# A two-block transformer and SSM kernel on one core: normed activations at another distance from the weights modulo 256 bytes, with three edits to the first layer and the SSD decays

## The chip, the core and the metric

The kernel runs on one core of one Trainium2 chip, in one launch. The metric is the device time of a launch in microseconds. All numbers of the profile are of one profiled execution.

## What is computed

The input `x` is 256 tokens of width 1024, in float32, with a context `ctx` of 256 tokens. Two blocks follow each other:

```
def first_block(x, ...):                 # two layers, h = h + layer(rms_norm(h))
    even: q, k, v, gate_a, u, gate_b = split(hn @ w_in)
          att = swa_sink_attention(rms(q), rms(k), v) * silu(gate_a)
          ssm = s5_mixer(u, log_dt, a, b, c, ...) * silu(gate_b)   # scan, then GLU
          out = concat(att, ssm) @ w_out
    odd:  q, k, v, gate, qi, ki, wi = split(hn @ w_in)
          out = (dsa_attention(q, k, v, qi, ki, wi) * silu(gate)) @ w_out

def second_block(x, c, ctx, c_ctx, ...):  # two layers, each: mixer, then a SwiGLU FFN
    sh1, sc1, g1, sh2, sc2, g2 = split(silu(c) @ ada_w + ada_b)    # and for ctx by c_ctx
    h = rmsnorm(x) * (1 + scale) + shift
    layer 0: attention of x over x and ctx (and of ctx over itself)
    layer 1: SSD mixer: z, xbc, dt = split(h @ w_in); conv; per head, in both
             directions, y = sum_j exp(-|cum_i - cum_j|) dt_j (C_i B_j) x_j + ...
    x = x + g1 * mixer;  x = x + g2 * swiglu(modulate(rmsnorm(x)))
    return rmsnorm(x)
```

`cum` is the running sum of `dt * A` of a head, `A = -exp(A_log)`. The weights come to about 260 MB in float32, and each is used once.

## The kernel before

**Dense products.** A weight tile `raw` of [128, 1024] float32 comes by DMA from SP. `Weights.load` (L171) splits it in two: ScalarE rounds it to `h` (L178), VectorE subtracts to get the rest, `l` (L179; GpSimd does so for the first `on_pool` tiles of a stage, counts in the list `LP`). The activations are split in the same way into H and L tiles of [128, 8, 256] (`nhx`, `nlx` for x, `nhc`, `nlc` for ctx, out of `norm_T`, L311; `yH`, `yL`, `oH`, `oL` out of the mixers; `fh`, `fl` within an FFN). Each product is then three matmuls: h with H, h with L, and l with H. All of them are recorded on line 129, in `mm`, so the tiles tell them apart. There are two forms. In the feature form (`feat_tiles`, L271) the weights are the stationary operand, and 256 columns of the activations move: `pu`, `pg`, `pffnx`, `pffnc`, `pcvx`. In the token form (`tok_step`, L229) a [128, 128] piece of the activations is stationary, and 256 or 512 columns of the weights move: `pdx`, `pdc`.

**Addresses.** Each partition holds its tiles at a fixed byte address. Modulo 256, the weights `h` and `l` lie at 224, the normed activations and the mixers' outputs at 160, an FFN's `fh` and `fl` at 160 (x) and 32 (ctx), the SSD's `ysH` at 32.

**Stages.** The even layer runs to about 330 us, with the adaLN rows (`pada`, from 512 KB tiles `araw` or `aw` of `ada_w`) and the ctx half of the second block's first layer in its holes; the odd layer to 515; the ctx FFN and the attention of x to 800; the first FFN of x to 1001; the SSD mixer `x_ssm` to 1362; the second FFN to 1557. What each engine does next is fixed in its own list of instructions by a scheduler, which goes by the program's order and by priorities; a `with after(mark)` holds what stands in it behind a marked instruction.

**First layer.** `norm_T` transposes x (`pntx`) and writes `nhx` (ScalarE, L334) and `nlx` (VectorE, L335). `late_params` (L358) brings small parameters into the tile `rp`, `A_log` among them, and makes `A = -exp(A_log)` by a power on GpSimd (L378) and steps L379 to L381 on VectorE. The S5 set-up makes its rotation tables from 16-column angle tiles `sv` on VectorE (L475 to L517, then `bb`, `bd`), and six table products `tabs` per quarter on GpSimd (L647 to L652). `cond_columns` (L860) makes `cT`, the silu of c and c_ctx, which every `pada` matmul needs; it is called at the head of `ctx_start`.

**SSD.** For each of eight groups of four heads, `project(g)` makes x, B and C (`pcvx`, then the convolution `cv`, `fT`) and z. `decay_rows(g)` fetches the rows of `cum` for the group into tiles `D_`, one per chunk of 128 tokens, and `decays(g)` makes the decay factors EW from them on GpSimd and ScalarE. It runs one group ahead:

```
G.tensor_tensor(D_, D_, negc[:, c, g, :, None] ..., op=ALU.subtract)   # L1396, 128x1024
S.activation(D_, D_, AF.Relu, scale=-1.0)                              # L1398, 128x1024
G: W = msk * dt (L1402, twice), W + Wb (L1403); E = D_0 + D_1 (L1405)
S.activation(E, E, AF.Exp, scale=-1.0)                                 # L1406
G.tensor_tensor(EW, E, W, op=ALU.mult)                                 # L1408
```

Ahead of some norms, a few warm matmuls (512 columns of float32 constants, counted as `pntx`) keep TensorE busy while it waits: two before the first FFN, five before the SSD, seven before the second FFN.

## Time and profile before

| what | value |
|---|---|
| median of 3 runs | 1563.68 us (1563.24 to 1567.5) |
| profiled execution, its own time | 1568.09 us |
| its span | 1566.3 us, mean granted clock 0.982 |
| TensorE matmul busy | 1484.5 us (95%) |
| VectorE, ScalarE, GpSimd busy | 1110.8, 770.8, 303.5 us (71%, 49%, 19%) |
| DMA | 264.56 MB, mean 169 GB/s |

The span is what the trace covers; the own time is what a launch took on the device. Idle time of an engine matters only where the end waits for it, so the shares are read first, then the chain that ended last, and then, for the stretches in question, busy time, waits and the groups of instructions.

### The profile page before, as it was taken

To read this page: it belongs to the slowest core of one execution; us is meant where nothing else is said; L and a number is where in the kernel's file an instruction comes from. 1 tells how busy PE (TensorE), PEld (TensorE's weight loads), DVE (VectorE), ACT (ScalarE), POOL (GpSimd) and SP (SyncE) were. 2 spreads that over 40 slices of the span, in tenths; PEclk is the share of its full clock that TensorE was granted. 3 is DMA by queue.
4 is the path that set the end of the run, shared out by engine and by line. 5 is a ranking of instruction groups with operands and counts; after the bars stand their busy time and mean duration, and the time that the engine had idled before them with its cause. 6 is when DMAs were issued, how large, how long until landed. Compare 5 with 4: busy or idle time off the path is not lost.

```text
span 1566.3 us, 26965 instructions
## 1 busy us (share of the span) xinstructions
PE 1484.5 (95%) x10560; PEld 1263.1 (81%) x10560; DVE 1110.8 (71%) x1825; ACT 770.8 (49%) x1386; POOL 303.5 (19%) x247
## 2 busy tenths in 40 slices
PE   6799999999999999999989999989899999999998
PEld 5574556786898888687779999888789898699997
DVE  6779996667766778666566666568988876665666
ACT  4433445654554555677444544445455544454444
POOL 2415660000100100000000000148975400200000
PEclk9899999999999999999999999998999999999999
DMA  9684555566665767642666465454544333556664
GB/s 254 228 233 142 184 173 164 139 182 200 200 180 172 223 192 212 217 121 95 209 203 192 162 185 180 141 134 125 125 112 131 105 95 122 159 161 188 193 189 134
DMA packets 306174, 264.56 MB, mean 169 GB/s; under 512 B 27441, under 2 KB 260703, under 8 KB 306048
## 3 DMA queue, kind: packets, MB, share of 16 engines
q1 hardware_dynamic: 306048, 262.85, 56.4%
q8 instruction: 83, 1.36, 0.4%
q14 instruction: 43, 0.35, 0.1%
HBM read 261.47 MB, written 1.34 MB: 168 GB/s over the span
## 4 chain that ended last, share of the span: by engine, by line
PE 78%; DVE 8%; DMA 5%; POOL 4%; ACT 2%; issue 2%; SPq 1%; POOLq 0%; DVEq 0%; ACTq 0%
PE pdx L129 21%; PE pffnx L129 16%; PE pdc L129 8%; PE pffnc L129 7%; PE pcvx L129 5%; PE pada L899 3%; PE pg L129 3%; DMA araw<-ada_w 2%; DVE l L179 2%; PE py L129 1%; PE pocx L129 1%; PE ptcx L1117 1%; PE pv L129 1%; POOL EW L1408 1%; PE pqi L129 1%
## 5 line engine op out<-in xcount | busy, mean ns | idle before, releaser
L179 DVE TENSOR_TENSOR l<-raw,h 128x1024 fp32r<-128x1024 f32 (+2 forms) x366 | 454.2, 1244 | 269.9 <-ACT h L178 239.0
L178 ACT ACTIVATE h<-raw 128x1024 fp32r<-128x1024 f32 (+2 forms) x374 | 389.0, 1042 | 412.3 <-PE pdx L129 103.2
L129 PE MATMUL pffnx<-nlx,h 128*128 128x256 f32 x704 | 169.6, 281 | 0.6 <-DVE nlx L354 0.6
L129 PE MATMUL pffnx<-nhx,h 128*128 128x256 f32 x704 | 169.7, 281 | 0.0
L129 PEld LDWEIGHTS pffnx<-nlx,h 128*128 128x128 f32 x704 | 133.8, 190 | 2.1 <-issue 1.2
L129 PEld LDWEIGHTS pffnx<-nhx,h 128*128 128x128 f32 x704 | 133.9, 190 | 0.5 <-issue 0.4
L308 POOL TENSOR_TENSOR sums<-sums,nhalf 128x1 f32<-128x1 f32 x20 | 13.0, 652 | 538.5 <-DVE sums L304 525.4
L129 PE MATMUL pffnx<-nhx,l 128*128 128x256 f32 x704 | 97.1, 280 | 0.0
L129 PE MATMUL pffnc<-nhc,h 128*128 128x256 f32 x352 | 88.9, 287 | 0.4 <-ACT nhc L353 0.4
L129 PEld LDWEIGHTS pffnx<-nhx,l 128*128 128x128 f32 x704 | 88.4, 189 | 0.8 <-issue 0.8
L129 PE MATMUL pffnc<-nlc,h 128*128 128x256 f32 x352 | 87.9, 285 | 0.1
L179 POOL TENSOR_TENSOR l<-raw,h 128x1024 fp32r<-128x1024 f32 (+1 forms) x8 | 18.5, 2314 | 352.3 <-PE pdx L129 199.5
L129 PE MATMUL pdx<-h,nhx 128*128 128x256 f32 (+1 forms) x256 | 83.3, 343 | 1.8 <-DVE cv L1290 1.8
L899 PE MATMUL pada<-araw,cT 128*32 128x256 f32 x704 | 71.8, 395 | 11.8 <-DMA araw<-ada_w 11.1
L129 PE MATMUL pdx<-h,nlx 128*128 128x256 f32 (+1 forms) x256 | 81.5, 336 | 0.0
L129 PE MATMUL pdx<-h,fh 128*128 128x256 f32 (+1 forms) x264 | 77.2, 318 | 0.0
L129 PE MATMUL pcvx<-nhx,h 128*128 128x256 f32 x256 | 73.5, 297 | 3.8 <-DVE cv L1290 3.8
L129 PE MATMUL pdx<-h,fl 128*128 128x256 f32 (+1 forms) x264 | 77.1, 317 | 0.0
L129 PE MATMUL pcvx<-nlx,h 128*128 128x256 f32 x256 | 71.5, 289 | 0.0
L129 PEld LDWEIGHTS pffnc<-nhc,h 128*128 128x128 f32 x352 | 66.5, 189 | 2.9 <-issue 1.2
L129 PEld LDWEIGHTS pffnc<-nlc,h 128*128 128x128 f32 x352 | 66.5, 189 | 2.1 <-DVE nlc L354 0.5
L129 PE MATMUL pdx<-l,nhx 128*128 128x256 f32 (+1 forms) x256 | 57.2, 338 | 1.4 <-DVE l L179 1.3
(622 smaller groups left out, 3884.2 us busy)
## 6 DMA issues: line engine op xcount, KB each, us to landing
araw<-ada_w SPq DMA_DIRECT2D x88, 512.0 KB
raw<-ffn_w_gate SPq DMA_DIRECT2D x66, 512.0 KB
raw<-ffn_w_up SPq DMA_DIRECT2D x66, 512.0 KB
raw<-ffn_w_down SPq DMA_DIRECT2D x54, 512.0 KB
raw<-ssm_w_in SPq DMA_DIRECT2D x48, 512.0 KB
raw<-od_w_in SPq DMA_DIRECT2D x25, 512.0 KB
raw<-attn_w_qkv SPq DMA_DIRECT2D x24, 512.0 KB
raw<-attn_w_o SPq DMA_DIRECT2D x32, 256.0 KB
```

What stands on the lines that cost most here:

```text
L129: i = T.matmul(out, l, r, start=start, stop=stop)
L178: S.activation(h[:, :n], raw[:, :n], AF.Copy)
L179: (G if self.on_pool > 0 else V).tensor_tensor(l[:, :n], raw[:, :n], h[:, :n].bitcast(F32), op=ALU.subtract)
L308: G.tensor_tensor(s[:, 3:4], s[:, j - 1:j], nhalf[:, 0:1], op=ALU.pow)
L899: T.matmul(pt[32 * q:32 * q + 32, 0:256], cT[:, k, :], raw[:, q * 256:(q + 1) * 256], start=k == 0, stop=k == 7, tile_position=(0, 32 * q))
L1117: T.transpose(pt[:, e, r], P[:, e, r, ki * 128:(ki + 1) * 128], ident)
L1408: G.tensor_tensor(EW, E, W, op=ALU.mult)
```

## The change

It has six parts.

1. **Addresses.** A helper `lane` makes the activation tiles 2112 elements wide, and uses 2048 of them from an offset of 60 (`nhx`, `nlx`, `nhc`, `nlc`) or 36 (`yH`, `yL`, `oH`, `oL`); a `pad` in `con`, and larger `hb`, `sink`, `padf`, `padk`, shift the rest. Modulo 256 the weights stay at 224. The normed activations go from 160 to 144, that is from 64 to 80 bytes below the weights; the mixers' outputs to 48; `fh`, `fl` of x to 32.
2. **First layer.** `cond_columns` is called right behind the first norm; the decay rates' part of `late_params` becomes `decay_rates`, called behind the odd layer; the first quarter's six table products wait for the first head norm's `rstd`.
3. **`LP[5]`** from 4 to 0: the first four `l` splits of the SSD are VectorE's.
4. **SSD decays.** GpSimd's subtraction of `cum` and the Relu become eight Relus of [128, 128] with a bias, and group 0's decays stand behind `project(0)`.
5. **Warm matmuls**: two, five and seven become none, four and six.
6. On SP, the two DMAs of `crows` (c and c_ctx) stand at places 8 and 9 of its list, and stood at 32 and 33; the DMA of `A_log` at 39, and stood at 27.

```
-LP = (0, 0, 2, 0, 2, 4)
+LP = (0, 0, 2, 0, 2, 0)
...
+    con.tile([128, 48], F32, name="pad")
...
+    def lane(tag, name, off):
+        t = act.tile([128, 2112], F32R, tag=tag, name=name)
+        return t[:, off:off + 2048].rearrange("p (k t) -> p k t", k=8)
...
-            G.tensor_tensor(r[:, :cnt], t[:, :cnt], nhalf[:, :cnt], op=ALU.pow)
+            i = G.tensor_tensor(r[:, :cnt], t[:, :cnt], nhalf[:, :cnt], op=ALU.pow)
+        marks.setdefault("rs" + key, i.ins)
...
-          H = act.tile([128, 8, 256], F32R, tag="h" + key, name="nh" + key)
-          L = act.tile([128, 8, 256], F32R, tag="l" + key, name="nl" + key)
+          H = lane("h" + key, "nh" + key, 60)
+          L = lane("l" + key, "nl" + key, 60)
...
+    def decay_rates():
+        ar = con.tile([64, 80], F32, name="ar")
+        a_diag, a_log, a_pos = ar[:, 0:64], ar[:, 64:65], ar[:, 65:67]
         SY.dma_start(a_log, dram(D("ssm_A_log_2"), 0, [[1, 64], [1, 1]]))
         G.tensor_tensor(a_pos[:, 0:1], ebase[0:64, 0:1], a_log, op=ALU.pow)
...
             wx.on_pool = LP[0]
+            cond_columns()
...
-            yH = act.tile([128, 8, 256], F32R, tag="hx", name="yH")
-            yL = act.tile([128, 8, 256], F32R, tag="lx", name="yL")
+            yH = lane("hx", "yH", 36)
+            yL = lane("lx", "yL", 36)
...
+                    with after(None if q else "rshe"):
+                        G.tensor_tensor(ct, hi(cos_), lo(cos_), op=ALU.mult)
...
+        if key == "x":
+            p.tile([128, 32], F32, name="padf")
...
-            ffn(p, wx, xt, i, 0, "x", psx, "xf", (11, 11), amid=amid, warm=(("endo", 2), ("ends", 7))[i])
+            ffn(p, wx, xt, i, 0, "x", psx, "xf", (11, 11), amid=amid, warm=((None, 0), ("ends", 6))[i])
...
-                    G.tensor_tensor(D_.rearrange("p d h i -> p (d h) i"), D_.rearrange("p d h i -> p (d h) i"),
-                                    negc[:, c, g, :, None].to_broadcast([128, 8, 128]), op=ALU.subtract)
-                    S.activation(D_, D_, AF.Relu, scale=-1.0)
+                    for d in range(2):
+                        for h in range(4):
+                            S.activation(D_[:, d, h], D_[:, d, h], AF.Relu, scale=-1.0,
+                                         bias=cum[:, 2 * c + d, 4 * g + h:4 * g + h + 1])
...
-            ew = decays(0, decay_rows(0))
+            row0 = decay_rows(0)
+            ew = None
...
-                EW = ew
+                EW = ew or decays(0, row0)
+    decay_rates()
```

**VectorE at the first norm.** Here `nlx` are the L halves of the first normed activations, `rp` the rates' steps, `sv` and `turn` the S5 angles, `cT` the conditioning columns. Before:

```order
L467 COPY ldx<-ldt 16x128
L335 SCALAR_TENSOR_TENSOR nlx<-pntx,par,nhx 128x256 x4
L471 COPY sv<-psp 128x48
L475 TENSOR_TENSOR sv<-sv 128x16
L480 TENSOR_TENSOR turn<-sv 128x16
L508 TENSOR_TENSOR sv<-sv 128x16
L379 TENSOR_SCALAR rp<-rp 64x1
L481 TENSOR_SCALAR turn<-turn 128x16
L335 SCALAR_TENSOR_TENSOR nlx<-pntx,par,nhx 128x256
L380 SCALAR_TENSOR_TENSOR rp<-rp 64x1
L483 CAST th_h<-turn 128x16
```

and now:

```order
L342 SCALAR_TENSOR_TENSOR nlx<-pntx,par,nhx 128x256
L478 COPY ldx<-ldt 16x128
L342 SCALAR_TENSOR_TENSOR nlx<-pntx,par,nhx 128x256
L883 TENSOR_SCALAR cT<-pcc 128x2x8
L342 SCALAR_TENSOR_TENSOR nlx<-pntx,par,nhx 128x256 x3
L482 COPY sv<-psp 128x48
L486 TENSOR_TENSOR sv<-sv 128x16
L491 TENSOR_TENSOR turn<-sv 128x16
L519 TENSOR_TENSOR sv<-sv 128x16
L492 TENSOR_SCALAR turn<-turn 128x16
L342 SCALAR_TENSOR_TENSOR nlx<-pntx,par,nhx 128x256
L494 CAST th_h<-turn 128x16
```

The steps on `rp` are gone from in front of the last `nlx`, and `cT`, which before stood at row 66 of this list, stands ahead of the last four.

**GpSimd at the same time.** `ldt`, `rp` (now `ar`) and `sv` are powers, `x` and `tabs` the table products, `t` and `r` a head norm's `rstd`. Before:

```order
L464 TENSOR_TENSOR ldt<-ebase,ld 16x2
L378 TENSOR_TENSOR rp<-ebase,rp 64x1
L476 TENSOR_TENSOR sv<-ebase,sv 128x16
L648 TENSOR_TENSOR x_196<-tr 128x512
L647 TENSOR_TENSOR tabs<-tr 128x512
L650 TENSOR_TENSOR tabs<-tr 128x512
L647 TENSOR_TENSOR tabs<-tr 128x512
L650 TENSOR_TENSOR tabs<-tr 128x512
L649 TENSOR_TENSOR tabs<-tabs,x_196 128x512
```

and now:

```order
L475 TENSOR_TENSOR ldt<-ebase,ld 16x2
L487 TENSOR_TENSOR sv<-ebase,sv 128x16
L388 TENSOR_TENSOR ar<-ebase,ar 64x1
L315 TENSOR_TENSOR sums<-sums,nhalf 128x1 x2
L292 TENSOR_SCALAR t<-ss 128x8
L293 TENSOR_TENSOR r<-t,nhalf 128x8
L659 TENSOR_TENSOR tabs<-tr 128x512
L660 TENSOR_TENSOR x_206<-tr 128x512
L662 TENSOR_TENSOR tabs<-tr 128x512
L659 TENSOR_TENSOR tabs<-tr 128x512
```

The power of `A_log` stands behind that of `sv`, and the first head norm ahead of the tables.

**ScalarE in the SSD's first group.** `cv` is the convolution's copy out of `pcvx`, `h` on L178 (now L184) the weights' split, `h_...<-phs` a state, and the `D_` rows are the decays. Before:

```order
L1437 ACTIVATE xf<-pxt 128x256
L1398 ACTIVATE D__10494<-D__10494 128x1024
L178 ACTIVATE h<-raw 128x1024
L1398 ACTIVATE D__10496<-D__10496 128x1024
L1406 ACTIVATE D__10494<-D__10494 128x512
L1362 ACTIVATE h_10832<-phs 128x512
L1287 ACTIVATE cv<-pcvx,par 128x512
L1406 ACTIVATE D__10496<-D__10496 128x512
```

and now:

```order
L1449 ACTIVATE xf<-pxt 128x256
L1368 ACTIVATE bc<-pct 128x128
L184 ACTIVATE h<-raw 128x1024
L1412 ACTIVATE D__10490<-D__10490,cum 128x128 x8
L1412 ACTIVATE D__10492<-D__10492,cum 128x128 x8
L1301 ACTIVATE cv<-pcvx,par 128x512
L1376 ACTIVATE h_10806<-phs 128x512
L1421 ACTIVATE D__10490<-D__10490 128x512
L184 ACTIVATE h<-raw 128x1024
```

Sixteen small Relus in two rows stand together, ahead of `cv` and the state's copy.

## Rows read from the trace of the kernel before

**Rows 1.** The page's first part: busy us, share of the span and instructions of each engine.

```profile
PE 1484.5 (95%) x10560; PEld 1263.1 (81%) x10560; DVE 1110.8 (71%) x1825; ACT 770.8 (49%) x1386; POOL 303.5 (19%) x247
```

**Rows 2.** Waits of TensorE, 0 to 70 us: total, times, longest.

```profile
PE pada L899 <- DVE cT L871: 5.0, 1, 5.0
PE pu L129 <- DVE nlx L335: 4.7, 2, 4.0
```

**Rows 3.** The chain that ended last, first 270 us: start, us, what.

```profile
20.13 2.25 DMA rp<-ssm_A_log
...
54.35 1.40 DVE bd L537
...
217.98 5.50 DMA araw<-ada_w
```

**Rows 4.** Timeline of VectorE: start, us, instruction, in brackets idle before and releaser.

```profile
23.01 0.15 DVE L379 TENSOR_SCALAR rp<-rp 64x1 f32<-64x1 f32 x1 [3.60 <-POOL rp L378]
...
34.41 0.16 DVE L515 TENSOR_TENSOR sv<-sv 128x16 f32<-128x16 f32 x1
...
37.72 0.98 DVE L511 TENSOR_TENSOR sv<-sv 128x16 f32<-128x16 f32 x1
...
43.66 0.17 DVE L871 TENSOR_SCALAR cT<-pcc 128x16 f32<-128x16 f32 x1
```

**Rows 5.** Windows: length; busy PE, PEld, DVE, ACT, POOL; clock, DMA share, GB/s.

```profile
20.00:50.00 30.00, 21.29 (x142) 17.35 (x143) 24.29 (x50) 9.81 (x14) 13.97 (x11) 0.77 0.83 293
50.00:80.00 30.00, 26.76 (x170) 18.64 (x169) 20.12 (x33) 14.28 (x21) 11.41 (x12) 0.89 0.70 221
80.00:108.00 28.00, 28.00 (x219) 24.80 (x218) 17.24 (x23) 12.19 (x14) 3.17 (x4) 1.00 0.85 229
```

**Rows 6.** The same view, windows of the SSD groups.

```profile
1042.00:1062.00 20.00, 15.00 (x97) 13.04 (x96) 13.08 (x19) 9.18 (x17) 12.15 (x9) 0.85 0.68 155
1062.00:1160.00 98.00, 86.91 (x656) 81.46 (x655) 85.75 (x108) 49.55 (x87) 88.54 (x61) 0.98 0.48 125
1160.00:1240.00 80.00, 74.75 (x585) 71.48 (x586) 69.67 (x110) 44.10 (x82) 41.19 (x31) 0.98 0.41 112
1240.00:1310.00 70.00, 70.00 (x561) 67.08 (x560) 54.49 (x99) 35.37 (x71) 7.55 (x8) 1.00 0.33 98
```

**Rows 7.** Lines L1396 and L1398 alone: durations in ns, min/median/max, and start.

```profile
L1396 POOL TENSOR_TENSOR D__10494<-D__10494,cumg x1: 1897/1897/1897, 1047.6 to 1047.6; 128x1024 f32<-128x1024 f32 x1
...
L1396 POOL TENSOR_TENSOR D__10940<-D__10940,cumg x1: 2875/2875/2875, 1090.3 to 1090.3; 128x1024 f32<-128x1024 f32 x1
...
L1398 ACT ACTIVATE D__10494<-D__10494 x1: 1059/1059/1059, 1049.5 to 1049.5; 128x1024 f32<-128x1024 f32 x1
```

**Rows 8.** Groups: ScalarE 1040:1310, VectorE 1042:1160, VectorE 300:800, GpSimd all.

```profile
L1436 ACT ACTIVATE bt<-pxt 128x128 f32<-128x128 f32 x16 | 4.4, 278 | 0.0
...
L179 DVE TENSOR_TENSOR l<-raw,h 128x1024 fp32r<-128x1024 f32 x17 | 28.8, 1701 | 6.5 <-ACT h L178 6.2 <-PE pct L1353 0.2
...
L179 DVE TENSOR_TENSOR l<-raw,h 128x1024 fp32r<-128x1024 f32 (+2 forms) x131 | 156.5, 1202 | 86.4 <-ACT h L178 82.1 <-PE pffnc L129 1.4 <-PE pdx L129 0.9
...
L179 POOL TENSOR_TENSOR l<-raw,h 128x1024 fp32r<-128x1024 f32 (+1 forms) x8 | 18.5, 2314 | 352.3 <-PE pdx L129 199.5 <-ACT h L178 151.3 <-issue 1.4
```

**Rows 9.** The chain again, at the FFNs and the SSD's head.

```profile
827.81 43.14 PE pffnx L129 x366
...
906.43 7.72 PE pffnx L129 x68
...
1001.81 4.56 PE pntx L129 x10
...
1465.49 62.19 PE pffnx L129 x528
```

**Rows 10.** The page's costliest groups, matmuls with normed activations moving.

```profile
L129 PE MATMUL pffnx<-nhx,h 128*128 128x256 f32 x704 | 169.7, 281 | 0.0
...
L129 PE MATMUL pffnc<-nhc,h 128*128 128x256 f32 x352 | 88.9, 287 | 0.4 <-ACT nhc L353 0.4
```

More of the change, by code (lines that the diff above doesn't have):

```diff
@@ L376, in late_params @@
             V.tensor_scalar(par[:, lo:hi], pp[:, lo:hi], 0.5, None, op0=ALU.mult)
+    def decay_rates():
+        ar = con.tile([64, 80], F32, name="ar")
+        a_diag, a_log, a_pos = ar[:, 0:64], ar[:, 64:65], ar[:, 65:67]
         SY.dma_start(a_log, dram(D("ssm_A_log_2"), 0, [[1, 64], [1, 1]]))
         G.tensor_tensor(a_pos[:, 0:1], ebase[0:64, 0:1], a_log, op=ALU.pow)
-        V.tensor_scalar(a_log, a_log, -e_del, 1.0, op0=ALU.mult, op1=ALU.add)
-        V.scalar_tensor_tensor(a_pos[:, 1:2], a_pos[:, 0:1], -1.0, a_log, op0=ALU.mult, op1=ALU.mult)
+        V.tensor_scalar(ar[:, 67:68], a_log, -e_del, 1.0, op0=ALU.mult, op1=ALU.add)
+        V.scalar_tensor_tensor(a_pos[:, 1:2], a_pos[:, 0:1], -1.0, ar[:, 67:68], op0=ALU.mult, op1=ALU.mult)
         V.tensor_scalar(a_diag, ident[0:64, 0:64], a_pos[:, 1:2], None, op0=ALU.mult)
@@ L646, in lo @@
                         return z[:, i4, 0:16][:, :, None, :].to_broadcast([128, 2, 16, 16])
-                    G.tensor_tensor(ct, hi(cos_), lo(cos_), op=ALU.mult)
-                    G.tensor_tensor(x1, hi(sin_), lo(sin_), op=ALU.mult)
-                    G.tensor_tensor(ct, ct, x1, op=ALU.subtract)
-                    G.tensor_tensor(sn, hi(sin_), lo(cos_), op=ALU.mult)
-                    G.tensor_tensor(x1, hi(cos_), lo(sin_), op=ALU.mult)
-                    G.tensor_tensor(sn, sn, x1, op=ALU.add)
+                    with after(None if q else "rshe"):
+                        G.tensor_tensor(ct, hi(cos_), lo(cos_), op=ALU.mult)
+                        G.tensor_tensor(x1, hi(sin_), lo(sin_), op=ALU.mult)
+                        G.tensor_tensor(ct, ct, x1, op=ALU.subtract)
+                        G.tensor_tensor(sn, hi(sin_), lo(cos_), op=ALU.mult)
+                        G.tensor_tensor(x1, hi(cos_), lo(sin_), op=ALU.mult)
+                        G.tensor_tensor(sn, sn, x1, op=ALU.add)
                     for j in range(2 * jj, 2 * jj + 2):
@@ L811, in odd_layer @@
             gate_feat(p, sg, [cols(w_in, NW, 1536 + c * 128) for c in range(8)], actk)
-            yH = act.tile([128, 8, 256], F32R, tag="hx", name="yHo")
-            yL = act.tile([128, 8, 256], F32R, tag="lx", name="yLo")
+            yH = lane("hx", "yHo", 36)
+            yL = lane("lx", "yLo", 36)
             scale = float(128 ** -0.5)
@@ L1171, in ctx_attend @@
         QT = cst_["QT"]
-        oH = act.tile([128, 8, 256], F32R, tag="hc", name="oHc")
-        oL = act.tile([128, 8, 256], F32R, tag="lc", name="oLc")
+        oH = lane("hc", "oHc", 36)
+        oL = lane("lc", "oLc", 36)
         def ada_tasks(u):
@@ L1218, in x_attention @@
                       lambda ci, m, pq, n0: qkv_evac(p, QT, KT, Vt, rope, psx, "x")((2, 0, 1)[ci], m, pq, n0), psx)
[L1219 to L1220 removed]
+            oH = lane("hx", "oHx", 36)
+            oL = lane("lx", "oLx", 36)
             vals = [Vc[:, 0], Vc[:, 1], Vt[:, 0], Vt[:, 1]]
@@ L1410, in decays @@
                 return out
-            negc = p.tile([128, 2, 8, 8], F32, name="cumg")
-            for c in range(2):
-                for d in range(2):
-                    V.tensor_copy(negc[:, c, :, 4 * d:4 * d + 4], cum[:, 2 * c + d].rearrange("p (g h) -> p g h", h=4))
-            ew = decays(0, decay_rows(0))
+            row0 = decay_rows(0)
+            ew = None
             for g in range(8):
```

13 lines of the change are left out of this document (5 added, 8 removed).

## The prediction

> **What bounds the kernel now.** I read the page's busy shares first [rows 1]: TensorE is busy for 1484.5 of 1566.3 us. So time can come from two places only: from the 82 us in which TensorE stands, or from the pace at which its matmuls follow each other. The stretches, the waits and the chain then say where it stands, the groups of instructions what one costs. Two places hold most of it that this change touches. In the first 80 us TensorE waits for the first layer's set-up [rows 2 to 5]; in the SSD groups between 1042 and 1240 us it works 176.7 of 198 us while GpSimd works 100.7 of the first 118 [rows 6]. From 1240 on it works 70.0 of 70 us: there nothing is to be had but pace.
>
> **First layer.** In 20 to 50 us TensorE works 21.3 of 30 us at a mean granted clock of 0.77, in 50 to 80 us 26.8 of 30 at 0.89 [rows 5]. That is 11.9 us of standing, and up to 30 x 0.23 + 30 x 0.11 = 10.2 us given away by the clock, part of which is at 1.2 GHz, the lower of its two levels, and falls there after such stops.
>
> One wait of 4.0 us (in the 4.7 of its row) is for the last `nlx` [rows 2]. The chain shows why: a DMA of `ssm_A_log` lands at 22.38 [rows 3], GpSimd raises it, VectorE's L379 stands idle for it until 23.01 [rows 4], and `nlx` is behind L379 on VectorE. The change takes GpSimd's power, the three VectorE steps and the DMA to a place behind the second layer. Nothing waits for `A_row` before the SSD's step sizes, so I cost them at nothing there: four steps of 0.15 to 0.6 us beside hundreds of microseconds of matmul. Gain 4.0; late next is TensorE's own list of `pu` matmuls.
>
> A second wait, 5.0 us, is for `cT` [rows 2]. It is a 0.17 us copy that VectorE reaches at 43.66 [rows 4]. The order now has it ahead of the last four `nlx`, since its two DMAs stand on SP as numbers 8 and 9 and not 32 and 33. What they are moved past on SP are small parameter loads, each two places later; `ssm_A_log` was the last of these, and it is gone, so SP's list is no longer there. Gain 5.0, and a supply of `pada` matmuls that fill later holes, as far as their own DMAs have come.
>
> Third, five [128, 16] steps of VectorE take about 1.0 us from 35.6 to 41 us (one shown) where the same shape takes 0.16 a moment before [rows 4]; GpSimd's six table products run just then. They are now held until the first head norm is out, and then have GpSimd nearly to themselves (3.2 of 28 us busy from 80 to 108 [rows 5]) before the scan needs them. That takes some 5 x 0.85 = 4.3 us off the chain to `bd`, which holds the chain for 1.4 us at 54.4 [rows 3]. So 4.0 + 5.0 + 1.4 = 10.4 us of waits can go, and with them part of 10.2 us of clock. Against this, the DMA engines are busy for 0.83 of 20 to 50 us [rows 5], and at 218 the chain is held by `araw` for 5.5 us [rows 3]: weights that need not come sooner. I take **-10** (bounds -3, where DMA keeps the rest, and -18, with three quarters of the clock).
>
> **SSD decays.** Per chunk GpSimd loses a 128x1024 subtraction of 1.90 to 2.88 us (16 of them, some 36 us), ScalarE's Relu of 1.06 us becomes eight of 128x128 [rows 7]. The nearest row, a 128x128 copy on ScalarE, takes 0.278 us [rows 8], so eight take 2.2, and ScalarE does 16 x 1.15 = 18 us more: 49.6 busy of 98 in 1062 to 1160 [rows 6] goes to some 61. VectorE has a second gain: its `l` split takes 1.70 us in 1042 to 1160, 1.20 in the dense stages without GpSimd [rows 8]. Upper bound: the standing of 1042 to 1240, 5.0 + 11.1 + 5.3 = 21.4 us, and half of some 6.6 us of lowered clock there (20 x 0.15, 98 x 0.02, 80 x 0.02): about -22 to -25. Lower bound: VectorE is busy for 85.8 of 98 us [rows 6] and becomes the limit, and the sixteen Relus in a row now stand in front of `cv` and `h` on ScalarE (order, third place), -4. Group 0's decays after `project(0)` cost nothing new: in either order they wait for the same DMA of `cum_s`, and `project(0)` is work that need not. I take **-14**: up to 1160 the twelve subtractions (some 26 us) leave GpSimd, but VectorE, busy for 98.8 of these 118 us, lets through 19 at most, of which I count a good half, -10; from 1160 on, where TensorE stands for 5.3, -4.
>
> **The small ones.** Four splits at the head of the SSD go from GpSimd (mean 2.31 us over all its splits) to VectorE (1.20) [rows 8]: 0, bounds +2 and -2, since VectorE's `dt` steps share that stretch. Warm matmuls: ten `pntx` took 4.56 us on the chain at 1001.8 [rows 9], so one of five is 0.9 us; `xn` comes late anyway, **-0.5**. In the last FFN `xn` is awaited behind them: 0. In the first FFN the two lie in a hole that waits for `araw`: 0, or +3 if the clock falls for want of them (20 x 0.15 by the row of 1042 [rows 6]).
>
> **The pace.** This is what the offsets can touch. The same 256-column matmul runs at two paces: 68 in 7.72 us are 113.5 ns each, 528 in 62.19 are 117.8 [rows 9]. Three pieces of `pffnx` (366, 460, 528; first and last shown) run slow, 1,354 of 2,112, or 64%. The paces hold for a whole piece, though activations and weights lie at the same distance modulo 256 in all of them; the paces change at small interruptions. So distance alone does not set the pace, and I take **0**. Bounds: the two FFN streams that read normed activations number 3 x (704 + 352) = 3,168 [rows 10]. At 4.3 ns, and 64% slow now, all fast is -8.7, all slow +4.9; for the SSD's and the 512-column ones I add a half: -13 to +7.
>
> The Trainium skill (SBUF — State Buffer, Who interferes with whom) speaks against any gain here: TensorE has a port of its own for the moving operand and one for the weights, and waits for no one. By that rule alone the term would be 0 and no second pace should exist; the two paces of the trace differ from it, so the rule does not close the question, and the sum rests on the rows.
>
> **Sum.** -10 - 14 - 0.5 + 0 = -24.5 on the profiled execution's 1568.1 us, that is 1543.6. This execution is 4.4 us above the median of the three, so against 1563.7 I say **1539**.
>
> **The rivals.**
> - *The pace locks fast.* For it: the two paces exist, and something in the relation of two address streams may choose; 80 is no multiple of 64, as all distances before were. Against: both paces occur at one distance. Sum -24.5 - 13: 1526. 30%.
> - *Savings are swallowed.* The first layer's work is paced by DMA (0.83 [rows 5], and 5.5 us at 218 [rows 3]), VectorE (85.8 of 98) by the time GpSimd is relieved. -3 - 4: 1557. 16%.
> - *ScalarE becomes the SSD's bound, slower.* Sixteen Relus in a row are 4.5 us in which no `cv`, `h` or `sz` leaves ScalarE. It decides where the next `cv` is ready during such a run; TensorE has two banks of `pcvx` and then stands. If every run lands on the path, 16 x 2.2 = 35 us are paid for at most 22 gained, +13, and each stop that lowers the clock costs 3 more, with one per group +24: +37 - 10 = 1590; with half of that 1572. For it: the third order excerpt. Against: ScalarE is busy for half the stretch only, and its relief from waiting for GpSimd's subtraction is part of the same edit. 7%.
> - The forecast itself (waits go, the offsets do nothing) has 47%. Its own range, by the bounds of its terms, is 1530 to 1551.
>
> **How the numbers follow.** About 0.3%, 4.7 us, is what a measurement of this kernel can tell from none. Faster by more: all of the forecast but 2, the fast pace, half of the swallowed case: 0.45 + 0.30 + 0.09 = 0.84. Within: 0.09. Slower: 0.07. The range goes from 1518 (fast pace and the first layer at -18) to 1558 (swallowed).
>
> **What would show it.** First layer: no wait of `pu` for `nlx` over 1 us, `cT` before 30 us, VectorE's small steps at 0.16, the wait at 218 still there. SSD: GpSimd under 0.7 busy in its groups, TensorE working over 95% of 1062 to 1240, ScalarE's 128 Relus at about 0.28 us. Pace: the long `pffnx` pieces at 117.8 in about two of three, as now; all at 113.5 means the first rival. TensorE waiting for `cv` L1301 of ScalarE means the third. A sum off by over 10 us with both stretches as forecast would make the pace term wrong.

## The result and the profile after

The change made the kernel **slower**: 1581.29 us in the median of five runs (1572.22 to 1585.28), against 1565.04 us (1563.24 to 1568.79) of the kernel before on the same chip; ratio 1.0092, 95% interval 1.0073 to 1.0111, some 14 us by the ratio and 16 by the two medians. The profiled execution took 1580.40 us, 12.3 more than the one of before, with a span of 1578.6 us and a mean granted clock of 0.981.

The page's first part, for [rows 1]:

```profile
PE 1501.7 (95%) x10552; PEld 1275.9 (81%) x10552; DVE 1088.6 (69%) x1825; ACT 793.7 (50%) x1498; POOL 265.1 (17%) x227
```

VectorE and GpSimd are relieved by 22 and 38 us, ScalarE has 23 more, as the edit of the decays says. But TensorE, which has eight instructions fewer, is busy for 17 us more, at the same mean clock (0.981, and 0.982 before). Busy time that grows with no instruction added means slower instructions, so the pace is read first. The chain that ended last, in the two FFNs of x and ahead of the SSD (start, us, what), for [rows 9]:

```profile
844.90 37.83 PE pffnx L135 x317
...
918.26 8.11 PE pffnx L135 x68
927.63 54.94 PE pffnx L135 x460
...
1014.69 3.70 PE pntx L135 x8
...
1477.61 62.96 PE pffnx L135 x528
```

All the `pffnx` pieces shown run at 119.2 to 119.4 ns per matmul (37.83 / 317, 54.94 / 460, 62.96 / 528). Before, the same 68 matmuls took 7.72 us (113.5 ns) and the same 528 took 62.19 (117.8). Neither of the two paces of before is left; a third one, slower than both, has taken their place. It is a mean: in the piece of 528 the step from one matmul's start to the next was 117 to 119 ns before, and runs through values from 116 to 124 ns after (start times of the two traces).

The first layer, for [rows 5], in the same windows (length; busy PE, PEld, DVE, ACT, POOL; clock, DMA share, GB/s):

```profile
20.00:50.00 30.00, 27.12 (x188) 21.70 (x187) 22.11 (x61) 14.30 (x20) 4.42 (x4) 1.00 0.89 327
50.00:80.00 30.00, 22.02 (x165) 16.55 (x164) 14.59 (x18) 10.79 (x16) 23.70 (x19) 0.89 0.77 247
80.00:108.00 28.00, 27.67 (x210) 22.65 (x208) 19.68 (x26) 11.06 (x14) 3.76 (x7) 1.00 0.87 219
```

From 20 to 50 us TensorE works 27.1 us instead of 21.3, at full clock instead of 0.77. From 50 to 80 it works 22.0 instead of 26.8: most of the gain is given back in the next 30 us. TensorE's waits up to 110 us (in total, times, longest) say to whom, for [rows 2]:

```profile
PE pqt L576 <- DVE qn L422: 6.4, 2, 4.5
...
PE pu L135 <- DVE nlx L342: 0.7, 1, 0.7
```

The wait for `nlx` is down from 4.7 to 0.7 and that for `cT` is gone; the one for `qn`, the normed q and k of the attention, stood at 2.2 before and is now 6.4. VectorE's timeline, for [rows 4], has both steps where the prediction wanted them, `cT` at 15 us and the small `sv` steps at 0.17:

```profile
15.46 0.16 DVE L883 TENSOR_SCALAR cT<-pcc 128x16 f32<-128x16 f32 x1
...
33.69 0.17 DVE L522 TENSOR_TENSOR sv<-sv 128x16 f32<-128x16 f32 x1
```

GpSimd's timeline shows what `qn` waits for (start, us, instruction, in brackets idle time before it and its releaser):

```profile
43.20 0.68 POOL L388 TENSOR_TENSOR ar<-ebase,ar 64x1 f32<-64x1 f32 x1 [20.64 <-DMA ar<-ssm_A_log]
...
55.49 0.20 POOL L292 TENSOR_SCALAR t<-ss 128x8 f32<-128x8 f32 x1 [9.15 <-DVE ss L420]
55.78 2.73 POOL L293 TENSOR_TENSOR r<-t,nhalf 128x8 f32<-128x8 f32 x1
58.48 1.04 POOL L659 TENSOR_TENSOR tabs<-tr 128x512 f32<-128x512 f32 x1
...
64.66 0.20 POOL L292 TENSOR_SCALAR t<-ss 128x8 f32<-128x8 f32 x1
...
66.56 1.64 POOL L293 TENSOR_TENSOR r<-t,nhalf 128x8 f32<-128x8 f32 x1
```

The table products, held until the first head norm's `r`, stand in front of the second one's. GpSimd is idle between 22 and 55 us but for two microseconds, and then the tables and both norms come at once. Before, the two long `r` started at 64.9 and 67.2 us: the first now comes 9 us earlier, the second 0.6.

The SSD, for [rows 6], with windows 12 us later:

```profile
1054.00:1074.00 20.00, 17.02 (x115) 15.43 (x114) 11.84 (x21) 12.33 (x32) 7.33 (x6) 0.91 0.56 156
1074.00:1172.00 98.00, 86.87 (x645) 82.10 (x645) 77.72 (x108) 64.78 (x158) 68.23 (x51) 0.97 0.45 127
1172.00:1252.00 80.00, 78.98 (x626) 75.89 (x625) 63.26 (x111) 48.97 (x110) 30.99 (x24) 1.00 0.45 124
1252.00:1322.00 70.00, 70.00 (x528) 66.10 (x527) 54.77 (x99) 34.17 (x67) 10.46 (x10) 1.00 0.30 91
```

In the second window GpSimd falls from 88.5 to 68.2 and VectorE from 85.8 to 77.7, and TensorE stays at 86.9. In the first and third it gains 2.0 and 4.2 us.

ScalarE's timeline at the head of that stretch, for [rows 7]:

```profile
1076.27 2.46 ACT L1412 ACTIVATE D__10494<-D__10494,cum 128x128 f32<-128x128 f32 x8 [4.93 <-DMA D__10494<-cum_s]
1078.63 0.40 ACT L1306 ACTIVATE fC<-cv 128x256 f32<-128x256 f32 x1
...
1080.71 2.45 ACT L1412 ACTIVATE D__10496<-D__10496,cum 128x128 f32<-128x128 f32 x8 [0.72 <-DMA D__10496<-cum_s]
1083.07 0.76 ACT L1301 ACTIVATE cv<-pcvx,par 128x512 f32<-128x512 f32 x1
```

ScalarE now waits 4.9 us at the head of its list for the rows of `cum`, with `fC`, `h` and `cv` behind it. Before, GpSimd's subtraction did that waiting. VectorE in turn waits for `cv` (waits of VectorE, 1054 to 1252), and its `l` split has not become much faster (groups of VectorE, 1054 to 1172), for [rows 8]:

```profile
DVE cv L1302 <- ACT cv L1301: 11.0, 5, 4.9
```

```profile
L185 DVE TENSOR_TENSOR l<-raw,h 128x1024 fp32r<-128x1024 f32 x18 | 30.1, 1671 | 12.4 <-ACT h L184 7.9 <-issue 2.9 <-PE pcvx L135 1.3
```

**Four stages.** To see where a kernel gains or loses, I cut its trace at three points that all kernels have: the first `pffnx`, and the last group of transposes in the norm ahead of the SSD and of the second FFN. On TensorE's timeline of the kernel after the latter two are

```profile
1020.12 1.06 PE L336 MATMUL pntx<-misc,xn 128*128 128x128 f32 x8 [0.85 <-DVE xn L351]
...
1379.59 1.94 PE L336 MATMUL pntx<-misc,xn 128*128 128x128 f32 x8 [0.86 <-DVE xn L351]
```

The lengths of the stages in one profiled execution each, in us, all read in this way. At the later two cuts all kernels have the same matmuls behind them but for warm ones; at the first they have not (start times: after and e1 have 24 `pdc` of ctx and 16 `pada` fewer done there than before, e3 has 42 and 32 fewer):

```
kernel           to first FFN  first FFN   SSD    second FFN   span
before               802.9       205.2    363.2     195.0     1566.3
after                810.5       209.6    359.5     199.0     1578.6
e1_no_offsets        805.5       203.6    356.1     195.7     1561.0
e2_offsets_only      806.6       207.4    365.0     199.1     1578.1
e3_no_hold           798.7       208.7    356.1     195.6     1559.1
e4_ssd_undone        806.7       203.9    362.2     195.6     1568.4
e5_ssd_only          804.1       204.8    356.1     195.5     1560.5
e6_alog_ssd          808.1       205.9    361.5     195.3     1570.9
e7_relu_split        804.6       205.4    371.7     198.4     1580.1
e8_splits4           802.8       204.3    365.2     195.0     1567.3
e9_splits12          806.7       204.7    358.6     196.5     1566.5
e10_rows_ahead       803.5       205.8    363.9     198.8     1572.0
```

After loses 4.4 and 4.0 us in the stages of the two FFNs of x, where no instruction was edited but for the warm matmuls, and gains 3.7 in the SSD. Its first FFN also holds those 40 matmuls, but so does that of e1, with 203.6 us. Up to the first FFN it is 7.6 late. One execution's stage moves by a few microseconds with periods of lowered clock (after has 0.93 from 110 to 270 us, e1 with the same instructions 0.97), so the medians of many runs decide, and the table says where to look. The kernel before is itself at 1565 to 1570 us by the chip that it runs on, so below the ratios are compared, each to before on the same chip.

### The profile page after: what moved, and what is told of

It reads as the page before. It is cut to its first block, busy times and chain, and to the rows that moved or that the text cites. A ratio compares the mean times of both kernels' runs of the same rounds, so it can differ in the third digit from the quotient of the medians.

```text
span 1578.6 us, 27033 instructions
## 1 busy us (share of the span) xinstructions
PE 1501.7 (95%) x10552; PEld 1275.9 (81%) x10552; DVE 1088.6 (69%) x1825; ACT 793.7 (50%) x1498; POOL 265.1 (17%) x227
## 4 chain that ended last, share of the span: by engine, by line
PE 80%; DVE 7%; DMA 6%; POOL 3%; ACT 2%; issue 1%; SPq 0%; POOLq 0%; ACTq 0%; DVEq 0%
PE pdx L135 22%; PE pffnx L135 16%; PE pffnc L135 8%; PE pcvx L135 7%; PE pdc L135 6%; PE pg L135 3%; PE pada L911 3%; DMA araw<-ada_w 2%; PE py L135 1%; DVE l L185 1%; DMA raw<-ev_w_in 1%; DVE m L680 1%; PE pocx L135 1%; PE ptcx L1131 1%; PE pglu L135 1%
## 5 line engine op out<-in xcount | busy, mean ns | idle before, releaser
L184 ACT ACTIVATE h<-raw 128x1024 fp32r<-128x1024 f32 (+2 forms) x374 | 389.8, 1043 | 430.3 <-PE pdx L135 114.7
L135 PE MATMUL pffnx<-nlx,h 128*128 128x256 f32 x704 | 173.8, 284 | 0.6 <-DVE nlx L361 0.6
L135 PE MATMUL pffnx<-nhx,h 128*128 128x256 f32 x704 | 173.8, 284 | 0.0
L911 PE MATMUL pada<-araw,cT 128*32 128x256 f32 x704 | 70.0, 402 | 10.9 <-DMA araw<-ada_w 10.3
L135 PEld LDWEIGHTS pdx<-h,nhx 128*128 128x128 f32 x256 | 49.8, 195 | 10.6 <-ACT h L184 3.1
```

Of the source, the lines that this page charges most:

```text
L135: i = T.matmul(out, l, r, start=start, stop=stop)
L184: S.activation(h[:, :n], raw[:, :n], AF.Copy)
L911: T.matmul(pt[32 * q:32 * q + 32, 0:256], cT[:, k, :], raw[:, q * 256:(q + 1) * 256], start=k == 0, stop=k == 7, tile_position=(0, 32 * q))
```

## Experiments

**Which part loses?** Theory: the addresses alone cost the time, by the pace. Rivals: the first layer's or the SSD's new order costs it. e1 is after with every tile back at its old address modulo 256 (the `pad` stays, as it makes good for the new tile `ar`), e2 is before with the address edits alone.

```
# e1, from after                              # e2, from before
-    t = act.tile([128, 2112], ...)           +def lane(tag, name, off): ...
+    t = act.tile([128, 2048], ...)           -H = act.tile([128, 8, 256], ...)
-    H = lane("h" + key, "nh" + key, 60)      +H = lane("h" + key, "nh" + key, 60)
+    H = lane("h" + key, "nh" + key, 0)       +yH = lane("hx", "yH", 36)
...                                           ...
```

> The changed kernel with its address edits undone: normed activations again 64 bytes below the weights modulo 256, mixers' outputs and FFN halves where they were before. Theory P (pace): 80 bytes below locks every feature-form stream of normed activations at about 119 ns per 256 columns; undone, a third of the matmuls run at 113 to 114 ns again and the time falls by 13 to 18 us against the changed kernel, to 1563 to 1568. Theory S (schedule): the loss is the first layer's new order; the time stays within 4 us of 1581.

> The kernel before with the address edits alone, its order of work untouched. Theory P: slower than before by 13 to 18 us, no pffnx matmul under 115.5 ns apart, median 119. Theory S: within 4 us of before.

e1: 1564.04 us against 1565.92, ratio 0.999 (0.9976 to 1.0004). e2: 1580.17, ratio 1.0089 (1.0059 to 1.0119). Both times came as theory P said. The addresses alone make the whole loss, and all the other edits together are worth nothing that can be told from zero. The chain has the paces. e1:

```profile
839.47 35.97 PE pffnx L135 x317
...
911.23 7.72 PE pffnx L135 x68
...
920.20 52.23 PE pffnx L135 x460
...
1460.24 62.19 PE pffnx L135 x528
```

e2:

```profile
920.66 54.94 PE pffnx L133 x460
...
1477.06 62.96 PE pffnx L133 x528
```

The piece of 460 before, which [rows 9] leave out:

```profile
915.41 54.26 PE pffnx L129 x460
```

It takes 52.23 us in e1 (113.5 ns each), 54.26 before (118.0), and 54.94 in e2 and after alike (119.4); the one of 528 takes 62.19, 62.19, and 62.96 twice. Since e1 and after have the same order, and before and e2 have another, the third pace goes with the address and not with the order. Which of the two old paces a piece runs at goes with the order: at 64 bytes e1, e3, e4 and e6 run the 460 at 113.5 ns, before and e5 at 118.0, and every one of them the 528 at 117.8. That is luck of the order, and it favours e1: its mean `pffnx` step is 114.6 ns, and 116.3 before and in e5, some 3 us over the 2112 of them that no edit was meant to bring.

From the start times: the steps of all 256-column matmuls at full clock that last 100 to 135 ns exceed 113.5 ns by 18.5 us in sum before, 33.1 after, 15.0 in e1 and 32.8 in e2. So after has 14.6 us more of it than before, and e2 14.3: nearly the whole loss. By mean steps, 2112 `pffnx` by 3.0 ns are 6.3 us, 1056 `pffnc` by 2.8 are 3.0, 1344 `pcvx` by 3.3 are 4.4, the rest is other streams.

**Does another distance do better?** Theory G: only the distance modulo 64 bytes counts, so multiples of 64 are alike and all others are slow. Theory M: each distance has a pace of its own. Eight kernels take e3 (below; old addresses) and move the normed activations of x and of ctx by other offsets, so that each gives two distances:

```
-    H = lane("h" + key, "nh" + key, 0)
+    H = lane("h" + key, "nh" + key, {"x": 12, "c": 48}[key])    # d3
```

> e3_no_hold with the normed activations of x at distance 0 from the weights modulo 256 and those of ctx at +32. One look for the pace of 256-column matmuls. Theory G (granule): only the distance within 64 bytes counts; 0 behaves as -64 (two paces, 113 to 114 and 117 to 118), +32 has one pace of its own, slower or faster than 116. Rival M: each distance modulo 256 has its own pace, and 0 and -64 differ.

> The same with x at -32 and ctx at +64. Theory G: x at -32 goes as ctx at +32 did, ctx at +64 has the two paces. Rival M: no such pairs.

> The same with x at -16 and ctx at +128. Theory G: -16 is 48 modulo 64, as -80 is, so x runs at about 119.2; ctx at +128 has the two paces. Rival M: x at -16 differs from 119.

> The same with x at -48 (16 modulo 64) and ctx at -96 (32 modulo 64). Theory G: ctx as at +32; x at -48 at a pace of its own, the one residue of the four that the other runs don't show; if the two-pace lock is broken on its fast side there, under 114.5 throughout and some 10 us less. Rival M: -96 differs from +32.

> e3_no_hold with x at -112 and ctx at +16 modulo 256, one look for the pace. By the distances tried so far (-64 and +64 two paces of 113 to 114 and 118; 0, -16, -32, -48, -80, -96, +32, +128 mixtures with means of 117 to 120) theory M says means of 117 to 120 at both; a mean under 114.5 at one would be a lock on the fast pace.

> The same with x at +80 and ctx at +96. Theory M: means of 117 to 120 at both. If sign doesn't matter, +80 goes as -80 (119.2) and +96 as -96 (118.3); a mean under 114.5 would be a lock on the fast pace.

> e3_no_hold with x at +48 and ctx at +112: with these, every distance that is a multiple of 16 has been looked at. Theory M: means of 117 to 120 at both, so that -64 and +64 stay the only ones with the fast pace in long pieces.

> e3_no_hold with x at -60 and ctx at -68, one element to either side of -64. If the two paces belong to an alignment to 64 bytes, both go to mixtures with means of 117 to 120; if to a neighbourhood, both keep long pieces at 113 to 114.

One execution of each d kernel, beside before on the same chip (for d1 to d4 one execution of it, else a median); e3 and after are medians. "x at" is the distance of `nhx` and `nlx` from the weights modulo 256 in bytes, "ctx at" that of `nhc` and `nlc`; the ns are the two long `pffnx` pieces of the chain divided by their 460 and 528:

```
kernel   x at  ctx at   us       before    ns (460)  ns (528)
(e3)     -64    -64     1562.37  1565.92    113.5     117.8
(after)  -80    -80     1581.29  1565.04    119.4     119.2
d1         0    +32     1577.86  1570.49    120.2     120.0
d2       -32    +64     1574.09  1570.49    118.5     118.3
d3       -16   +128     1573.42  1570.49    117.3     117.1
d4       -48    -96     1578.22  1570.49    119.3     116.7
d5      -112    +16     1577.83  1569.61    118.8     118.7
d6       +80    +96     1584.86  1569.61    120.2     120.0
d7       +48   +112     1577.52  1568.82    118.5     118.3
d8       -60    -68     1585.22  1568.82    121.3     121.1
```

The two ends of the list are d3 and d8. d3:

```profile
920.87 53.97 PE pffnx L135 x460
...
1471.48 61.85 PE pffnx L135 x528
```

d8:

```profile
927.11 55.79 PE pffnx L135 x460
...
1480.89 63.95 PE pffnx L135 x528
```

G falls on both sides: distance 0, a multiple of 64, runs at 120, and -16 and -48, which are none, beat 117.8 in the last piece. M is left, though not one pace to a distance: -48 has two as well (119.3 and 116.7), and 0 and +80 agree. The weights lay at 224 in all of these kernels, so the runs cannot tell the distance from the address of the activations alone. Four bytes beside -64, in d8, give the slowest pace of all. For ctx, by the start times, the mean step between `pffnc` matmuls goes from 115.8 ns (+112) to 119.6 (+96), with 115.8 to 116.4 at -64 by the order; and of x's long pieces only those at -64 reach 113.5. All eight keep all else of e3, and came in 0.2% to 1.0% over the kernel before where e3 came in 0.2% under it. One execution cannot tell 0.2% from none, but the mean `pffnx` step, 117.2 (d3) to 121.1 ns (d8) for 114.6 in e3, says the same: none of the offsets that were tried helps x. Finer ones, and other addresses for the weights, were not tried.

**The first layer.** Theory: the hold on the table products gives the gain of the first 60 us back. Rival: the gain is lost to work that must come anyway, hold or no hold. e3 is e1 without the hold; e6 is e3 with `cond_columns` back in its old place as well.

```
-                    with after(None if q else "rshe"):     # e3
+                    with after(None):
...
-            cond_columns()                                 # e6, behind the first norm
     def ctx_start():
+        cond_columns()
```

> As e1_no_offsets, but the first quarter's table products on GpSimd are not held behind the first head norm. Theory H: the hold puts the second head norm's reciprocal root behind the tables on GpSimd (TensorE waits 4.5 us for qn), and the tables' later half into VectorE's attention stretch; without it the first layer ends 4 to 10 us earlier than in e1_no_offsets. Rival D: that stretch is paced by DMA of ada_w and VectorE; within 3 us of e1_no_offsets.

> As e3_no_hold, but the conditioning columns are made where they were before, so of the first layer's edits only the move of A_log is left. Theory F: within 3 us of e5_ssd_only and e3_no_hold, with the wait of pu for nlx gone and the wait for cT back. Rival C: the early cT itself costs, by ctx work drawn ahead of x's, and this is 3 us or more under e3_no_hold; or it gains, and this is 3 us or more over it.

e3: 1562.37 us, ratio 0.9979 (0.9964 to 0.9995). e6: 1569.81, ratio 0.9987 (0.9966 to 1.0007). The hold costs some 1.7 us (e1 against e3), not told from zero, as their intervals overlap: rival D's outcome, and not the 4 to 10 us of theory H. In e3 TensorE's wait for `qn` falls to

```profile
PE pqt L576 <- DVE qn L422: 3.5, 1, 3.5
```

but the even layer does not end much earlier for that: the first matmul of the odd layer's index queries (`pqi`) starts at 323.4 us before, 323.5 in e1, 322.1 in e3 and 323.7 in e5, which has none of the first layer's edits. The lead on x's chain is there at first: the first S5 matmul (`py`) starts at 90.3 us in e3 and at 104.8 before, but the last at 247.8 and 250.3. In between the chain of e3 waits for `araw` where that of before did, at 217.98 for 5.50 us [rows 3]:

```profile
217.72 6.15 DMA araw<-ada_w
```

Later x's chain is ahead again, at the cost of other work. In e3 the odd layer's attention has its first product with v (`poo`) at 447.0 us, and before at 458.6. First before, then e3:

```profile
L129 PE MATMUL poo<-PT,Vto x12: 592/592/697, 458.6 to 509.7; 128*128 128x512 f32 x12
...
L129 PE MATMUL pffnc<-nlc,h x352: 276/281/387, 395.3 to 739.9; 128*128 128x256 f32 x176
```

```profile
L135 PE MATMUL poo<-PT,Vto x12: 592/592/697, 447.0 to 495.6; 128*128 128x512 f32 x12
...
L135 PE MATMUL pffnc<-nlc,h x352: 276/281/386, 406.0 to 760.2; 128*128 128x256 f32 x176
```

So x's own chain is 11.6 us ahead. But the FFN of ctx has its last `pffnc` with `nlc` at 760.2, where before it had it at 739.9: what x gained, ctx lost and more. From 323 to 803 us TensorE is busy for 470.8 of 480 us in e3 and for 471.2 before (windows), so there are no holes left for work that is put off. The first FFN starts at 798.7 us in e3, 805.5 in e1, and 802.9 before, but with 42 `pdc` and 32 `pada` fewer done than before. They come in the FFN's stage (208.7 us for 205.2), and at the SSD's head, with equal work, e3 is 0.7 us ahead, with the piece of 460 faster by 2.0. How much of the lead DMA took and how much ctx work did was not told apart. e6 came as theory F said (within 3 us of e3 and e5, the wait for `cT` back with 4.9 us) and settles nothing beyond that: its ratio is level with both, and its profiled execution, at 1572.66 us the slowest of its runs, needs 361.5 us for the same SSD that takes 356.1 in e3.

**The SSD.** Theory: the edit gains some 14 us, which e1 and after hide behind losses elsewhere. Rival: it gains little by itself. e4 is e1 with the SSD of before, e5 is before with the SSD edits, `LP` and the warm matmuls alone (parts 3 to 5).

```
# e5, from before (e4 is the reverse, from e1)
-LP = (0, 0, 2, 0, 2, 4)
+LP = (0, 0, 2, 0, 2, 0)
-    G.tensor_tensor(D_ ..., negc ..., op=ALU.subtract)
-    S.activation(D_, D_, AF.Relu, scale=-1.0)
+    for d in range(2):
+        for h in range(4):
+            S.activation(D_[:, d, h], D_[:, d, h], AF.Relu, scale=-1.0, bias=cum[...])
-    ew = decays(0, decay_rows(0))
+    row0 = decay_rows(0)
```

> As e1_no_offsets, but with the SSD's decays, its first four splits on GpSimd and the fifth warm matmul as in the kernel before. Theory: the SSD part gains 6 to 9 us (less standing and less lowered clock, as the traces differ), so this is 6 to 9 us slower than e1_no_offsets. Rival: ScalarE's 128 small Relus cost what GpSimd's subtraction gave; within 3 us.

> The kernel before with the SSD part alone: small Relus, four splits on VectorE, fewer warm matmuls. Addresses and first layer as before. Theory F: the first layer's edits save TensorE no standing in all, they move it (the lead of 7 to 9 us at 60 us is gone at 250), while the SSD part gains about 5: this runs 4 to 7 us under the kernel before, level with e3_no_hold or up to 2 us faster. Rival: e3_no_hold keeps a first-layer gain of 3 us or more, and this is that much slower than it.

e4: 1569.45 us, ratio 1.0016 (1.0 to 1.0032), so the SSD's edits gain 0.26% in e1, some 4 us, which is between the 6 to 9 of its theory and the 3 of its rival. e5: 1565.09, ratio 0.9969 (0.9957 to 0.998), a gain of 0.31%, or 4.9 us, as theory F said. In the table of stages, e1, e3 and e5 all have 356.1 us of SSD where before has 363.2 (e5's profiled execution, at 1562.25 us, is the fastest of its ten). The windows of e5 from 1062 on show where it is not:

```profile
1062.00:1160.00 98.00, 86.29 (x666) 81.59 (x665) 76.80 (x113) 65.67 (x160) 69.24 (x52) 0.97 0.50 132
1160.00:1240.00 80.00, 77.71 (x625) 74.54 (x624) 62.94 (x111) 49.32 (x111) 31.69 (x26) 1.00 0.45 119
```

TensorE's 86.3 us of the first window were 86.9 before [rows 6], with GpSimd and VectorE relieved by 19 and 9 us. From 1160 on it gains 3.0.

**Is ScalarE's list what holds it?** Theory A: yes, since the Relus stand ahead of `cv`, `fC` and `h`. Rival V: VectorE, which passes every `cv` and `l` on, is the one with no slack. e7 takes half of the Relus off ScalarE: for the second direction VectorE makes min(D - cum, 0), and GpSimd's sum becomes a difference.

```
+    if d:
+        V.tensor_scalar(D_[:, d, h], D_[:, d, h], cc, 0.0, op0=ALU.subtract, op1=ALU.min)
+    else:
         S.activation(D_[:, d, h], D_[:, d, h], AF.Relu, scale=-1.0, bias=cc)
-    G.tensor_tensor(E, E, D_[:, 1], op=ALU.add)
+    G.tensor_tensor(E, E, D_[:, 1], op=ALU.subtract)
```

> As e5_ssd_only, but the four Relus of the backward direction of each chunk are done by VectorE (subtract cum, minimum with 0), and GpSimd subtracts that half instead of adding it. Theory A: the SSD part gained 5 us and not 14 because runs of eight Relus (2.45 us) and their wait for the rows' DMA hold cv, fC, h and the weights' split on ScalarE; halved, TensorE waits 2 to 6 us less for ScalarE, and the time is 0.1 to 0.4% under e5_ssd_only's ratio of 0.9969. Rival V: VectorE, busy for 77 of 98 us there, is the limit; the same ratio or above it.

e7: 1577.11 us, ratio 1.0042 (1.0023 to 1.0061), 0.7% slower than e5. Its window, in a profiled execution that is the slowest of its six (1581.86 us):

```profile
1062.00:1160.00 98.00, 83.52 (x580) 78.35 (x580) 79.61 (x141) 50.53 (x114) 67.78 (x51) 0.88 0.47 121
```

ScalarE falls by 15 us, VectorE rises by 3, and TensorE loses 2.8 us of work and a tenth of its clock; its longest waits are now for VectorE (`PE pcvx L129 <- DVE cv L1290: 6.5, 4, 3.0`, from 1042 to 1240 us). A falls in this form: fifteen microseconds less on ScalarE brought nothing. That the few more on VectorE are what costs, as V has it, is not shown: the clock, and the new order that comes with the edit, may have their part.

**The four splits.** The prediction put part 3 at nothing. e8 gives GpSimd its four `l` splits of the SSD back, e9 gives it twelve.

```
-LP = (0, 0, 2, 0, 2, 0)
+LP = (0, 0, 2, 0, 2, 4)      # e8
+LP = (0, 0, 2, 0, 2, 12)     # e9
```

> As e5_ssd_only, but the SSD's first four weight splits stay on GpSimd, as in the kernel before: part 3 of the change undone alone. Rival V (VectorE limits the SSD): 0.1 to 0.2% under e5_ssd_only's ratio of 0.9969. Theory N: those splits lie ahead of the groups, beside work that TensorE has; within 0.1% of it.

> As e5_ssd_only, with the first twelve splits on GpSimd, which the decays' subtraction has left free. If VectorE is the limit in the first groups, 3 to 6 us under e5_ssd_only (a ratio of 0.993 to 0.995); if GpSimd's 2.3 us per split, or its reads beside VectorE's, put it on the path, level with e5_ssd_only or slower.

e8: 1570.22 us, ratio 1.0012 (0.9993 to 1.0032): the whole gain of e5 is gone. e9: 1563.0, ratio **0.9959** (0.9942 to 0.9975), the lowest of all, its interval overlapping that of e5. Neither came as forecast: e8 is slower than both V and N have it, e9 lies between its two cases. Four is worse than none, twelve is not, so the load of VectorE or GpSimd alone does not explain it. The waits of TensorE in e8, 1042 to 1240 us, do show its place:

```profile
PE phx L129 <- ACT h L1362: 15.5, 5, 3.7
```

`h` of L1362, the state's copy, stands on ScalarE behind Relus that wait for their rows. Before, this wait was 3.6 us in all, and in e5 5.1. With another list the same Relus come to stand elsewhere, and the state waits or doesn't. This fits the loss; no run moved the Relus alone.

**The rows two groups ahead.** e10 is e9 with the DMAs of the `cum` rows issued one group sooner, into four tiles per chunk instead of two: the lateness of the rows should go, the work stays.

```
-DB = 2
+DB = 4
-            row0 = decay_rows(0)
+            drows = [decay_rows(0), decay_rows(1)]
...
-                nrow = decay_rows(g + 1) if g < 7 else None
+                if g < 6:
+                    drows.append(decay_rows(g + 2))
```

> As e9, but the rows of cum are fetched two groups ahead instead of one (four tiles D_ per chunk pair instead of two). Theory A, that what is left of the SSD's expected gain is lost in ScalarE's queue, where a group's Relus stand first in line and wait for the DMA of their rows: some 20 us of ScalarE waits for DMA of cum_s go, TensorE's waits for cv and h behind them shorten, and the time falls by 2 to 5 us under e9: ratio to the kernel before 0.992 to 0.995. Rival, that these waits lie in holes of ScalarE that nobody pays for (ScalarE is busy for two thirds of that stretch): the ScalarE waits go, TensorE's busy share of 1062 to 1160 us stays, ratio 0.995 to 0.997. Slower than e9 by over 0.2% would say that the order of the list, which shifts with every edit, outweighs both.

e10: 1570.74 us, ratio 1.0004 (0.999 to 1.0019), 0.45% slower than e9. ScalarE's waits for these rows, summed over the SSD, are 25.4 us in after, 23.0 in e9 and 14.5 in e10; it was GpSimd that had them before, with 17.1. So 8.5 us of them went, and the time did not fall. The windows at the SSD's head, in profiled executions that lie 5 us (e9) and 3 us (e10) above their kernels' medians; e9, then e10:

```profile
1042.00:1062.00 20.00, 18.38 (x142) 16.72 (x140) 9.03 (x15) 14.49 (x36) 13.15 (x8) 1.00 0.59 137
1062.00:1160.00 98.00, 86.26 (x654) 82.01 (x655) 76.80 (x106) 65.18 (x159) 75.99 (x55) 0.95 0.51 135
```

```profile
1042.00:1062.00 20.00, 15.84 (x116) 14.07 (x115) 7.62 (x16) 16.79 (x47) 13.40 (x9) 1.00 0.78 205
1062.00:1160.00 98.00, 84.00 (x626) 78.90 (x624) 77.69 (x107) 65.07 (x161) 75.51 (x55) 0.95 0.49 131
```

Two groups of rows now come at once at the head (DMA share 0.78 for 0.59), TensorE does 2.5 us less there and 2.3 less in the next window. Its waits in e10 are for VectorE (from 1030 to 1330 us):

```profile
PE phs L129 <- DVE xc L1356: 7.8, 3, 3.8
PE pcvx L129 <- DVE cv L1290: 3.9, 2, 3.2
PE phx L129 <- ACT h L1362: 2.7, 1, 2.7
```

The theory that the rows' waits hold the rest falls in this form, and so does its first rival, by which the time would have stayed at that of e9; the third outcome named ahead, slower by over 0.2%, is what came; it was to mean that a shift of the list outweighs both, but the rows' DMAs at the head may have their part. Why one list is 5 us better than another stays open: it was not shown for any single wait.

## Why the prediction was wrong

It said 1539 us, faster by 24.5. The result is slower by 14 us. Of the 38 us between them the addresses make some 14 (e2), and the other edits some 23, since they brought 1.6 us (e1) and not 24.5.

- **The pace** is the step that failed, and the one that turned a gain into a loss. The prediction took 0 between -13 and +7, and its upper bound was "all slow +4.9" with half as much again: it took the two paces that the trace of before showed for all that there are. They are those of one distance. At 80 bytes there is a third, 119.3 ns, and the streams affected cost some 14 us (e2 by itself 1.0089). The sentence "distance alone does not set the pace" was right for 64 bytes and wrong as a reason for 0: a trace made at one distance cannot bound another. The rival that was missing is "all streams at a pace slower than any seen"; its price could not have been read from the rows of before, which should have made the upper bound wide. The forecast's own range of 1530 to 1551 is also narrower than its terms: the bounds of the two large ones alone span 1521 (-18 and -25) to 1557 (-3 and -4).
- The Trainium skill (SBUF — State Buffer, Who interferes with whom) gives TensorE two independent ports, and the Trainium skill (TensorE: Matmul & The Clock Gate, Step-by-step: what each phase is for) says that loading the next weights "doesn't steal SBUF read bandwidth from the running matmul". The runs differ from what one would draw from both: the same matmul with the same weight load takes 116.7 to 121.3 ns by the address of the activations at the distances tried, and 113.5 or 117.8 at -64 by the order. What in the memory does this was not shown.
- **First layer, -10 forecast.** Each wait went as said: `nlx` 0.7, `cT` at 15.5 us, small steps at 0.17. The step that failed is "4.0 + 5.0 + 1.4 = 10.4 us of waits can go" as a gain of the end. By 110 us TensorE has done 600 matmuls, and 579 before; by 323 us it is 1698, and 1752 before (1747 in e3): the lead is gone before the odd layer. What x gains again later, as e3 shows, ctx work loses. The wait at 218 is still in e3's chain; in after's it is not, with `araw` waits at 247 and 254 instead. Late next was not "TensorE's own list of `pu` matmuls" but `qn`, behind a head norm that the hold puts with the tables into the same 15 us of GpSimd. All first-layer edits together cost 3.3 us (e1 against e5, by their ratios), without the hold 1.6 (e3 against e5), neither told from zero with certainty, and both with the luck of the faster `pffnx` pieces, some 3 us, on their side.
- **SSD, -14 forecast.** Right in sign, mis-sized: -4.9 by e5's ratio, -7.1 in the profiles' stage. The -4 from 1160 us on came (74.8 to 77.7 us of work in e5, 79.0 after). The -10 before it did not, and that is the step that failed here: it was counted on VectorE's relief, "lets through 19 at most, of which I count a good half". VectorE was relieved by 8 to 9 us and GpSimd by 19 to 20, and TensorE stayed at 86.3 to 86.9 of 98. A second gain was to come from `l` at 1202 ns; `l` went from 1701 to 1671 (1555 in e5) only, and VectorE's new waits are for `cv` of ScalarE (11.0 us). Eight Relus took 2.45 us instead of 2.2. GpSimd is at 0.70 busy, as said; TensorE at 93.2% of the two windows (165.9 of 178), not over 95%.
- **The four splits, 0 within 2.** Mis-sized: with the new decays e5 is 0.43% faster than e8, some 6.7 us. As twelve on GpSimd (e9) cost nothing, this is not the price of a split, and the prediction had no term for the order of the lists.
- **Warm matmuls, -0.5.** As said: eight take 3.70 us, ten took 4.56, and nothing is lost in the first FFN (204.8 us in e5, 205.2 before).
- **The rivals.** Fast pace: no. Savings swallowed: half right, as the first layer's were. DMA's part is open: TensorE's own waits for `araw` come to 10.3 us after and 11.1 before, but e3's chain still waits for it at 218; ctx work put off is the part that was seen. ScalarE as the SSD's bound: its mark, waits for `cv`, is there on VectorE, but the SSD became shorter and e7 speaks against it as the bound. Slower came with none of them.

## What to carry to other kernels

A term that rests on one address, one order or one size has no bound from a trace made at that value alone; where it touches some 4,500 matmuls, 3 ns each are 14 us, more than the other edits brought together. So try the address edit by itself before three others are put on top of it. A wait that TensorE loses early is a gain only if the next shared point moves too, with as much work behind it: compare starts and counts of matmuls done, and not sums of waits. In a stretch with four engines in turn, moving work off the busiest may just move the place at the head of a queue where a late DMA is awaited; edits that moved a few rows of a list were worth 5 us or more here (e8, e10).
